# A written, pinned matrix-engine order for the stick-breaking attention of a two-block model

## The chip, the cores and the metric

The kernel runs on one core of a Trainium2 chip. The metric is the device time of one execution, in microseconds (us). The engines of the core work side by side, each through its own queue in order: TensorE (PE, matrix products; PEld is its weight load), VectorE (DVE), ScalarE (ACT), GpSimd (POOL) and SyncE (SP, which issues the transfers).

## The reference

Two transformer-like blocks on 512 tokens of width 1024, in float32. The change lies in the mixer of the second block, in its stick-breaking attention with 16 heads of 64:

```python
def stick_breaking_attention(q, k, v):   # (B, H, S, Dh)
    # A[t,s] = beta_ts * prod_{s<j<t}(1-beta_tj), s<t
    for i in range(s_ // SB_BLOCK):      # blocks of 128 query rows
        z = jnp.einsum('bhtd,bhsd->bhts', qb, kb) * scale
        log_1mb = jnp.where(causal, jax.nn.log_sigmoid(-z), 0.0)
        suffix = lax.cumsum(log_1mb, axis=3, reverse=True) - log_1mb
        log_a = jnp.where(causal, jax.nn.log_sigmoid(z) + suffix, -jnp.inf)
        a = jnp.exp(log_a)
        outs.append(jnp.einsum('bhts,bhsd->bhtd', a, vb))
...
    o_att = rmsnorm(stick_breaking_attention(heads(q), heads(k), heads(v)), attn_norm_g)
    return jnp.concatenate([o_att, o_ssd], axis=-1) @ w_out
```

## The kernel before

Every large product is made of split operands: a float32 number is kept as a high and a low part (`whi`, `wlo` for weights, `a_hi`, `a_lo` for activations) in a format that PE multiplies fast, and three products (high by high, low by high, high by low) are summed in one bank of PSUM. `split` (L79) makes the high part on ACT (L82, or L85 with a factor) and the low part on DVE (L83, or L86). `wload` (L102) fetches a piece of a weight matrix through SP into one of three `raw` buffers and splits it; `whi` and `wlo` have two buffers each.

The attention goes by eight pairs of heads. For each pair `proj_T` makes Q and K, transposed, from the activations: 8 steps of 3 matmuls of 512 columns each (L164), 48 matmuls for a pair, into the banks mm 0 and 1. Q and K are split (L85, L86 and L82, L83) into qh, ql, kh, kl and put into place by 12 transfers on SP (L1056, L1059). Then come three units of query rows (`GROUPS`: blocks 0 and 1 together, block 2, block 3). A unit has, for each of two heads, the scores (L1070, high and low K; for the third unit 512 columns each), a sigmoid l on ACT (L1074), and a running product E along the keys on DVE (L1079, a scan). A unit's E is then turned by PE transposes in float32 (L1087), copied out of PSUM as aT by ACT for the first head and by DVE for the second (L1094, L1096, L1098), and multiplied with V (L1027, values, float32) into the bank `ob`. The values of a unit are held back and issued after the transposes of the next one, so that the float32 products of PE come together in a run; `after` adds dependences that keep it so. The first head's transposes go to a bank `tp`, the second's to bank mm 3. The third unit's values close a pair: ACT adds a row (oaF, L1035) and squares it (q2, L1040), DVE sums the squares (sq, L1041).

V is stored as differences of neighbouring tokens: SP fetches the rows shifted by one into a buffer (L960, L961, L966) and DVE subtracts (L967). Two buffers serve the four row tiles.

After the last pair, zs (the output of the other half of the mixer, of L971 to L983) is transposed on PE (L236) and split, and `w_out` follows in chunks of 24 matmuls (L209, 512 columns each), eight for each half of the output's columns. Of a half's eight, the first four use the transposed zs (a_hi, a_lo) and the others the attention output (oat_hi, oat_lo), which needs the norm over all heads: the sum of squares over partitions (L1111), L1115 to L1120, and for each pair of heads a product on DVE (L1124) and a split.

The order of each engine's instructions is set before the run by a scheduler that takes the instructions in the written order and moves them where its own estimate finds a gap; an instruction marked `keep_in_program_order` isn't moved past others so marked. At run time each engine keeps its order and waits where an operand or a buffer isn't ready.

## Time and profile before

| | |
|---|---|
| time, median of 3 runs | 1955.44 us (1954.67 to 1955.9) |
| the profiled execution | 1953.41 us, its span 1951.6 us |
| PE busy | 1903.7 us, 98% of the span |
| PE weight load busy | 1556.5 us, 80% |
| DVE busy | 982.8 us, 50% |
| ACT busy | 721.8 us, 37% |
| the stick-breaking stretch, first to last score | about 1153.7 to 1310 us of the span |

The span is the time from the first to the last instruction of the profiled execution. A busy PE is not PE at its peak, since matmuls overlap and their ends are modelled. The granted clock is that of PE: 1.00 is 2.4 GHz and 0.50 is 1.2 GHz. Idle time of an engine is named with the instruction that ended it.

### The profile page before, as it was taken

To read this page: it belongs to the slowest core of one execution; us is meant where nothing else is said; L and a number is where in the kernel's file an instruction comes from. 1 tells how busy PE (TensorE), PEld (TensorE's weight loads), DVE (VectorE), ACT (ScalarE), POOL (GpSimd) and SP (SyncE) were. 2 spreads that over 40 slices of the span, in tenths; PEclk is the share of its full clock that TensorE was granted. 3 is DMA by queue.
4 is the path that set the end of the run, shared out by engine and by line. 5 is a ranking of instruction groups with operands and counts; after the bars stand their busy time and mean duration, and the time that the engine had idled before them with its cause. 6 is when DMAs were issued, how large, how long until landed. Compare 5 with 4: busy or idle time off the path is not lost.

```text
span 1951.6 us, 24228 instructions
## 1 busy us (share of the span) xinstructions
PE 1903.7 (98%) x9677; PEld 1556.5 (80%) x9677; DVE 982.8 (50%) x1681; ACT 721.8 (37%) x1246; POOL 38.3 (2%) x66
## 2 busy tenths in 40 slices
PE   7999999999999999999999999999999999999998
PEld 6778888788878888888877877767788888888887
DVE  5578833724553333324668755665464553333223
ACT  4345533233333323223445434544353432323221
POOL 0000000100000000000000000000000000000000
PEclk9999999999999999999999999999999999999999
DMA  7411133232332333333321445442262312333322
GB/s 245 130 44 34 34 97 97 87 98 86 108 97 87 98 97 97 98 97 119 89 82 50 128 121 136 128 120 76 87 194 78 105 57 86 97 98 97 97 97 86
DMA packets 154336, 193.21 MB, mean 99 GB/s; under 512 B 9976, under 2 KB 111732, under 8 KB 154096
## 3 DMA queue, kind: packets, MB, share of 16 engines
q1 hardware_dynamic: 154224, 191.66, 32.7%
q8 instruction: 76, 1.25, 0.3%
q14 instruction: 36, 0.29, 0.0%
HBM read 174.85 MB, written 2.10 MB: 91 GB/s over the span
## 4 chain that ended last, share of the span: by engine, by line
PE 84%; DVE 8%; ACT 1%; issue 1%; POOL 1%; DMA 1%; POOLq 0%; DVEq 0%; ACTq 0%
PE mm L164 43%; PE mm L209 27%; PE mm L187 3%; DVE E L1079 1%; DVE x_sb L279 1%; POOL rp_r L76 1%; PE ob L538 1%; DVE h L251 1%; PE ob L1027 1%; PE s L561 1%; PE ob L924 1%; PE s L1182 1%; PE s L1070 1%; DVE fg L272 1%; PE mm L579 1%
## 5 line engine op out<-in xcount | busy, mean ns | idle before, releaser
L83 DVE TENSOR_TENSOR wlo<-raw,whi 128x1024 fp32r<-128x1024 f32 (+1 forms) x274 | 333.6, 1218 | 680.3 <-ACT whi L82 675.0
L82 ACT ACTIVATE whi<-raw 128x1024 fp32r<-128x1024 f32 (+1 forms) x274 | 289.0, 1055 | 687.3 <-PE mm L164 289.9
L164 PE MATMUL mm<-a_hi,wlo 128*128 128x512 f32 x1120 | 438.0, 391 | 1.6 <-DVE wlo L83 1.6
L164 PE MATMUL mm<-a_hi,whi 128*128 128x512 f32 x1120 | 438.9, 392 | 0.0
L164 PE MATMUL mm<-a_lo,whi 128*128 128x512 f32 x1120 | 438.5, 392 | 0.0
L164 PEld LDWEIGHTS mm<-a_hi,wlo 128*128 128x128 f32 x1120 | 210.3, 188 | 44.5 <-DVE wlo L83 2.0
L164 PEld LDWEIGHTS mm<-a_lo,whi 128*128 128x128 f32 x1120 | 210.3, 188 | 44.0 <-issue 2.4
L164 PEld LDWEIGHTS mm<-a_hi,whi 128*128 128x128 f32 x1120 | 210.3, 188 | 43.3 <-issue 1.4
L209 PE MATMUL mm<-whi,a_hi 128*128 128x512 f32 (+1 forms) x384 | 151.2, 394 | 2.3 <-ACT a_hi L82 2.3
L209 PE MATMUL mm<-whi,a_lo 128*128 128x512 f32 (+1 forms) x384 | 151.7, 395 | 0.0
L209 PE MATMUL mm<-wlo,a_hi 128*128 128x512 f32 (+1 forms) x384 | 150.0, 391 | 0.0
L209 PE MATMUL mm<-whi,hid_hi 128*128 128x512 f32 x288 | 112.0, 389 | 0.0
L209 PE MATMUL mm<-whi,hid_lo 128*128 128x512 f32 x288 | 112.0, 389 | 0.0
L209 PE MATMUL mm<-wlo,hid_hi 128*128 128x512 f32 x288 | 112.0, 389 | 0.0
L209 PEld LDWEIGHTS mm<-whi,a_hi 128*128 128x128 f32 x384 | 72.9, 190 | 19.0 <-ACT a_hi L82 3.1
L209 PEld LDWEIGHTS mm<-whi,a_lo 128*128 128x128 f32 x384 | 72.9, 190 | 15.4 <-issue 2.5
L209 PEld LDWEIGHTS mm<-wlo,a_hi 128*128 128x128 f32 x384 | 72.8, 190 | 14.5 <-issue 1.8
L76 POOL TENSOR_TENSOR rp_r<-rp_a,half 128x1 f32<-128x1 f32 (+1 forms) x58 | 36.9, 636 | 1887.5 <-DVE rp_a L74 1565.0
L209 PEld LDWEIGHTS mm<-whi,hid_lo 128*128 128x128 f32 x288 | 54.1, 188 | 11.3
L209 PEld LDWEIGHTS mm<-wlo,hid_hi 128*128 128x128 f32 x288 | 54.1, 188 | 11.2
L209 PEld LDWEIGHTS mm<-whi,hid_hi 128*128 128x128 f32 x288 | 54.1, 188 | 11.2
L1079 DVE TENSOR_TENSOR_SCAN E<-l,own 128x128 f32<-128x128 f32 (+2 forms) x64 | 48.6, 809 | 10.9 <-ACT l L1074 10.9
(452 smaller groups left out, 2844.8 us busy)
## 6 DMA issues: line engine op xcount, KB each, us to landing
raw<-in_w_in_dram SPq DMA_DIRECT2D x96, 512.0 KB, 3.8
raw<-in_ffn_w_gu_dram SPq DMA_DIRECT2D x88, 512.0 KB, 3.6
raw<-in_ffn_w_down_dram SPq DMA_DIRECT2D x44, 512.0 KB, 3.7
raw<-in_w_out_dram SPq DMA_DIRECT2D x24, 512.0 KB, 3.7
raw<-in_xa_wkv_dram SPq DMA_DIRECT2D x16, 512.0 KB, 4.3
raw<-in_w_ret_o_dram SPq DMA_DIRECT2D x8, 512.0 KB, 3.4
K<-kh SPq DMA_DIRECT2D x32, 128.0 KB, 2.3
K<-kl SPq DMA_DIRECT2D x32, 128.0 KB, 2.3
```

The source lines that it names most:

```text
L76: POOL.tensor_tensor(r[:, :n], a[:, :n], half[:, :n], op=ALU.pow)
L82: ACT.activation(hi, src, AF.Copy)
L83: V.tensor_tensor(lo, src, hi.bitcast(F32), op=ALU.subtract)
L164: PE.matmul(o, a, b, start=(kc + k == 0 and n == 0 and si == 0), stop=(kc + k == K - 1 and n == 2), skip_group_check=True)
L187: PE.matmul(banks[g][j][:, t0 * 128:t1 * 128], a, b, start=(kc + k + n + si == 0), stop=(kc == 1 and k == 3 and n == 2), skip_group_check= ...
L209: PE.matmul(banks[t][:, :w], a, b, start=(kk == 0 and n == 0), stop=(kk == K - 1 and n == 2))
L251: V.scalar_tensor_tensor(h, src, r, g, op0=ALU.mult, op1=ALU.mult)
L272: V.tensor_tensor(fgt, bank, gpost[:, hf * 512:(hf + 1) * 512], op=ALU.mult)
L279: V.scalar_tensor_tensor(xs, fg[:, t if q == 0 else NT + t % 2], r, xs, op0=ALU.mult, op1=ALU.add)
L538: m = PE.matmul(ob[64 * e:64 * e + 64, a], vv[:, j, br, g * 64:(g + 1) * 64], pT[:, e, j], start=False, stop=(br == 1 and j == nk - 1), sk ...
L561: PE.matmul(sbs[e], qS[:, h, qsl], kk[:, br, g, :W], start=(n == 0 and (e == 0 or nk > 2)), stop=(n == 1), skip_group_check=True)
L1079: last = V.tensor_tensor_scan(E[:, rev], l[:, rev], own1[:, 511:(511 - W) if W < 512 else None:-1], 1.0, op0=ALU.mult, op1=ALU.max)
```

## The change

Three things are changed.

First, V's differences get four buffers in place of two (two of them in a free region, `bcT`), and the subtractions are written behind the two steps that make z, two behind each.

Second, the PE instructions of pairs 0 to 6 are written in the order in which they are to run and pinned in it (`pe` marks matmuls and transposes). A generator `projections` yields after each 3 projection matmuls. 28 of its steps go ahead of the first score (Q and K of pair 0, Q of pair 1, half of K of pair 1). Then `ORDER` is followed for each pair: `s` is the scores of one unit and head, `R` a run (the transposes of a unit's two heads, and the values of the unit before), `.` three projection matmuls, sixteen of them in a pair. The third unit's scores stand behind the first unit's run.

Third, pair 7 isn't pinned; there the dependences of `after` stay. The projections end in pair 6.

```diff
@@ -953,19 +953,15 @@
             return f
         for c in range(2):
             proj_X(w, 2048 + c * 512, 512, get, ev_v(c))
-        vbefore = lambda t: d1.tile([128, D], F32, name="vbefore", tag=("xdt", "xdec")[t % 2])
-        vb = vbefore(0)
-        V.memset(vb[0:1], 0.0)
+        vb2 = d1.tile([128, 2, D], F32, name="vb2", tag="bcT")
+        vb = [d1.tile([128, D], F32, name="vb0", tag="xdt"), d1.tile([128, D], F32, name="vb1", tag="xdec"), vb2[:, 0], vb2[:, 1]]
+        V.memset(vb[0][0:1], 0.0)
         for t in range(NT):
-            nc.sync.dma_start(vb[1:113], vv[0:112, t])
-            nc.sync.dma_start(vb[113:128], vv[112:127, t])
-            nxt = None
+            nc.sync.dma_start(vb[t][1:113], vv[0:112, t])
+            nc.sync.dma_start(vb[t][113:128], vv[112:127, t])
             if t < NT - 1:
                 nc.sync.dma_start(vl[t * 8 + 8:t * 8 + 16], vv[127:128, t].rearrange("o (p c) -> o p c", p=8))
-                nxt = vbefore(t + 1)
-                nc.sync.dma_start(nxt[0:1], vv[127:128, t])
-            V.tensor_tensor(vv[:, t], vb, vv[:, t], op=ALU.subtract)
-            vb = nxt
+                nc.sync.dma_start(vb[t + 1][0:1], vv[127:128, t])
 
 
         zs = l1.tile([128, NT, D], F32, name="zs", tag="u3")
@@ -987,6 +983,8 @@
             return t[:, 0], t[:, 1]
         for g in range(2):
             proj_X(w, 3072 + g * 512, 512, get, ev_z(g), tail=2, slots=[spare])
+            for t in range(2 * g, 2 * g + 2):
+                V.tensor_tensor(vv[:, t], vb[t], vv[:, t], op=ALU.subtract)
         tp = tpp.tile([128, 4, 128], F32, name="tp")
         PE.transpose(tp[:, 0, 0:32], vl, ident[0:32, 0:32])
         vlT = l1.tile([128, NT, 8], F32, name="vlT")
@@ -1024,8 +1022,8 @@
                 for i, j, n, o in pv:
                     for e in range(2):
                         h = 2 * p + e
-                        m = PE.matmul(ob[64 * e:64 * e + 64, i * 128:(i + n) * 128], vv[:, j, h * 64:(h + 1) * 64], aTs[e][:, o:o + n],
-                                      start=(i == 0), stop=(n == 2 or j == i), skip_group_check=True)
+                        m = pe(PE.matmul(ob[64 * e:64 * e + 64, i * 128:(i + n) * 128], vv[:, j, h * 64:(h + 1) * 64], aTs[e][:, o:o + n],
+                                         start=(i == 0), stop=(n == 2 or j == i), skip_group_check=True))
                         if first:
                             after(m, *others)
                             first = False
@@ -1041,67 +1039,109 @@
                         V.tensor_tensor(sq, sq, q2, op=ALU.add)
             return f
 
+
+        pinned = [True]
+
+        def pe(m):
+            return tc.keep_in_program_order(m) if pinned[0] else m
+        QK = {}
+
+        def projections():
+
+            for p in range(8):
+
+                Q = qk.tile([128, 2, 512], F32R, name="Q")
+                K = [qk.tile([128, 2, 512], F32R, name=f"K{i}") for i in range(2)]
+                QK[p] = Q, K
+                for nm, c0, scale in (("q", 0, 0.125), ("k", 1024, None)):
+                    hi = a1.tile([128, 512], F32R, name=f"{nm}h")
+                    lo = a1.tile([128, 512], F32R, name=f"{nm}l")
+                    wh, wl = wload(w, 0, 8, c0 + p * 128, 128)
+                    o = bank((0, 1))
+                    for k in range(8):
+                        xh, xl = get(k, 0, NT)
+                        for n, (a, b) in enumerate(((wh, xh), (wh, xl), (wl, xh))):
+                            pe(PE.matmul(o, a[:, k], b, start=(k + n == 0), stop=(k == 7 and n == 2), skip_group_check=True))
+                        if k == 7:
+                            split(hi, lo, o, scale)
+                            for r in range(2):
+                                for e in range(2):
+                                    rows = slice(64 * e, 64 * e + 64)
+                                    if nm == "q":
+                                        nc.sync.dma_start(Q[64 * r:64 * r + 64, e].bitcast(F32), (hi, lo)[r][rows].bitcast(F32))
+                                    else:
+                                        for i, x in enumerate((hi, lo)):
+                                            nc.sync.dma_start(K[i][64 * r:64 * r + 64, e].bitcast(F32), x[rows].bitcast(F32))
+                        yield
+        stream = projections()
+
+        def steps(n):
+            for _ in range(n):
+                next(stream, None)
+
+        def score(p, segs, e):
+
+            Q, K = QK[p]
+            T = segs[-1][1] + (segs[-1][0] + 1) * 128
+            sb = score_bank(p)
+            first = True
+            for i, off in segs:
+                W = (i + 1) * 128
+                for n, k in enumerate(K):
+                    pe(PE.matmul(sb[:, off:off + W], Q[:, e, i * 128:(i + 1) * 128], k[:, e, :W], start=first, stop=(n == 1),
+                                 skip_group_check=True))
+                    first = False
+            l = a2.tile([128, 512], F32, name="l", bufs=3)
+            ACT.activation(l[:, :T], sb[:, :T], AF.Sigmoid, scale=-1.0)
+
+            E = a2.tile([128, 512], F32, name="E", bufs=5)
+            for off, W in (((0, 128), (128, 256)) if len(segs) == 2 else ((0, T),)):
+                rev = slice(off + W - 1, (off - 1) if off else None, -1)
+                last = V.tensor_tensor_scan(E[:, rev], l[:, rev], own1[:, 511:(511 - W) if W < 512 else None:-1], 1.0,
+                                            op0=ALU.mult, op1=ALU.max)
+            return E, last
+
+        def turned(p, segs, Es, last):
+
+            n = segs[-1][1] // 128 + segs[-1][0] + 1
+
+            own, rest = (slice(0, 3, 2), slice(1, 2)) if len(segs) == 2 else (slice(n - 1, n), slice(0, n - 1))
+            aTs = []
+            for e in range(2):
+                tp = tpp.tile([128, 4, 128], F32, name="tp") if e == 0 or p == 7 else bank((3,)).rearrange("p (j q) -> p j q", j=4)
+                for j in range(n):
+                    m = pe(PE.transpose(tp[:, j], Es[e][:, j * 128:(j + 1) * 128], ident))
+                    if e + j == 0 and not pinned[0]:
+                        after(m, last)
+                aT = a2.tile([128, 4, 128], F32, name="aT", bufs=4)
+                (V.tensor_copy if e else ACT.copy)(aT[:, rest], tp[:, rest])
+                if e:
+                    V.tensor_scalar(aT[:, own], tp[:, own], -1.0, None, op0=ALU.add)
+                else:
+                    ACT.activation(aT[:, own], tp[:, own], AF.Identity, bias=less1)
+                aTs.append(aT)
+            if held:
+                held.pop()(*(() if pinned[0] else (last,)))
+            if segs is GROUPS[0]:
+                obs[0] = op_.tile([128, 512], F32, name="ob")
+            held.append(values(p, segs, aTs, obs[0]))
+        obs = [None]
+        steps(28)
+
+        ORDER = "sss.s..Rs.sR...R.........".replace(" ", "")
         for p in range(8):
-
-            Q = qk.tile([128, 2, 512], F32R, name="Q")
-            K = [qk.tile([128, 2, 512], F32R, name=f"K{i}") for i in range(2)]
-            for nm, c0, scale in (("q", 0, 0.125), ("k", 1024, None)):
-                hi = a1.tile([128, 512], F32R, name=f"{nm}h")
-                lo = a1.tile([128, 512], F32R, name=f"{nm}l")
-                proj_T(w, c0 + p * 128, 128, get, lambda j, bank, hi=hi, lo=lo, sc=scale: split(hi, lo, bank, sc), of=(0, 1))
-                for r in range(2):
-                    for e in range(2):
-                        rows = slice(64 * e, 64 * e + 64)
-                        if nm == "q":
-                            nc.sync.dma_start(Q[64 * r:64 * r + 64, e].bitcast(F32), (hi, lo)[r][rows].bitcast(F32))
-                        else:
-                            for i, x in enumerate((hi, lo)):
-                                nc.sync.dma_start(K[i][64 * r:64 * r + 64, e].bitcast(F32), x[rows].bitcast(F32))
-            ob = None
-            for segs in GROUPS:
-                T = segs[-1][1] + (segs[-1][0] + 1) * 128
-                css, last = [], None
-                for e in range(2):
-                    sb = score_bank(p)
-                    first = True
-                    for i, off in segs:
-                        W = (i + 1) * 128
-                        for n, k in enumerate(K):
-                            PE.matmul(sb[:, off:off + W], Q[:, e, i * 128:(i + 1) * 128], k[:, e, :W], start=first, stop=(n == 1),
-                                      skip_group_check=True)
-                            first = False
-                    l = a2.tile([128, 512], F32, name="l", bufs=3)
-                    ACT.activation(l[:, :T], sb[:, :T], AF.Sigmoid, scale=-1.0)
-
-                    E = a2.tile([128, 512], F32, name="E", bufs=5)
-                    for off, W in (((0, 128), (128, 256)) if len(segs) == 2 else ((0, T),)):
-                        rev = slice(off + W - 1, (off - 1) if off else None, -1)
-                        last = V.tensor_tensor_scan(E[:, rev], l[:, rev], own1[:, 511:(511 - W) if W < 512 else None:-1], 1.0,
-                                                    op0=ALU.mult, op1=ALU.max)
-                    css.append(E)
-
-                aTs = []
-                for e in range(2):
-                    tp = tpp.tile([128, 4, 128], F32, name="tp") if e == 0 or p == 7 else bank((3,)).rearrange("p (j q) -> p j q", j=4)
-                    for j in range(T // 128):
-                        m = PE.transpose(tp[:, j], css[e][:, j * 128:(j + 1) * 128], ident)
-                        if e + j == 0:
-                            after(m, last)
-                    aT = a2.tile([128, 4, 128], F32, name="aT", bufs=4)
-
-                    n = T // 128
-                    own, rest = (slice(0, 3, 2), slice(1, 2)) if len(segs) == 2 else (slice(n - 1, n), slice(0, n - 1))
-                    (V.tensor_copy if e else ACT.copy)(aT[:, rest], tp[:, rest])
-                    if e:
-                        V.tensor_scalar(aT[:, own], tp[:, own], -1.0, None, op0=ALU.add)
-                    else:
-                        ACT.activation(aT[:, own], tp[:, own], AF.Identity, bias=less1)
-                    aTs.append(aT)
-                if held:
-                    held.pop()(last)
-                if ob is None:
-                    ob = op_.tile([128, 512], F32, name="ob")
-                held.append(values(p, segs, aTs, ob))
+            pinned[0] = p < 7
+            todo = [(u, e) for u in range(3) for e in range(2)]
+            ES, runs = {}, list(range(3))
+            for c in ORDER:
+                if c == "s":
+                    u, e = todo.pop(0)
+                    ES[u, e] = score(p, GROUPS[u], e)
+                elif c == "R":
+                    u = runs.pop(0)
+                    turned(p, GROUPS[u], [ES[u, e][0] for e in range(2)], ES[u, 1][1])
+                elif p < 7:
+                    steps(1)
         held.pop()()
         osT = new_act()
         for t in range(NT):
```

On PE, in the second pair of heads (pair 1), from the third unit's scores to the second unit's transposes: `s` and `mm` are score banks, `tp` and `mm` with `E` the transposes of the first and the second head, `ob` the values, `mm<-a_..` the projections. Before:

```order
L1070 MATMUL s<-K_9152,Q 128x512
L1070 MATMUL s<-K_9153,Q 128x512
L1087 MATMUL mm<-cst,E 128x128
L1070 MATMUL mm<-K_9152,Q 128x512
L1087 MATMUL tp<-cst,E 128x128 x3
L1087 MATMUL mm<-cst,E 128x128 x2
L1027 MATMUL ob<-aT,vv 64x128 x8
L1087 MATMUL tp<-cst,E 128x128 x3
L1070 MATMUL mm<-K_9153,Q 128x512
L1087 MATMUL mm<-cst,E 128x128 x3
```

Now, from the first unit's transposes:

```order
L1113 MATMUL tp<-cst,E 128x128 x3
L1113 MATMUL mm<-cst,E 128x128 x3
L1025 MATMUL ob<-aT,vv 64x128 x8
L1091 MATMUL s<-K_9048,Q 128x512
L1091 MATMUL s<-K_9049,Q 128x512
L1064 MATMUL mm<-a_hi,whi 128x512
L1064 MATMUL mm<-a_lo,whi 128x512
L1064 MATMUL mm<-a_hi,wlo 128x512
L1091 MATMUL mm<-K_9048,Q 128x512
L1091 MATMUL mm<-K_9049,Q 128x512
L1113 MATMUL tp<-cst,E 128x128 x3
L1113 MATMUL mm<-cst,E 128x128 x3
```

The third unit's scores moved from ahead of the first unit's transposes to behind its run, with three projection matmuls between their two heads, and the pieces of a run stand together.

On PE, from the third unit's transposes of pair 6 on (`mm<-cst,zs` are the transposes of zs, `mm<-whi,a_hi` and the like matmuls of w_out). Before:

```order
L1087 MATMUL tp<-cst,E 128x128 x4
L1087 MATMUL mm<-cst,E 128x128 x4
L1027 MATMUL ob<-aT,vv 64x128 x6
L164 MATMUL mm<-a_lo,whi 128x512
L164 MATMUL mm<-a_hi,wlo 128x512
L236 MATMUL mm<-cst,zs 128x128 x12
L209 MATMUL mm<-whi,a_hi 128x512
L236 MATMUL mm<-cst,zs 128x128 x8
L209 MATMUL mm<-whi,a_lo 128x512
```

Now:

```order
L236 MATMUL mm<-cst,zs 128x128 x5
L1113 MATMUL tp<-cst,E 128x128 x4
L236 MATMUL mm<-cst,zs 128x128 x3
L1113 MATMUL mm<-cst,E 128x128 x4
L1025 MATMUL ob<-aT,vv 64x128 x6
L236 MATMUL mm<-cst,zs 128x128 x4
L209 MATMUL mm<-whi,a_hi 128x512
L236 MATMUL mm<-cst,zs 128x128 x3
L1091 MATMUL s<-K_10227,Q 128x128
```

The transposes of zs, before all behind the pair's last projection, now begin ahead of the third unit's transposes, and pair 7's first score stands behind 15 of them.

On DVE, behind pair 7: the norm (`rstd`), the scaled heads (`oaF`), their splits (`oat_lo`) and the weight splits of w_out (`wlo`). Before:

```order
L1118 TENSOR_TENSOR rstd<-rstd 128x512
L83 TENSOR_TENSOR memT_lo<-tp,memT_hi 128x512
L1119 SCALAR_TENSOR_TENSOR rstd<-rstd 128x512
L83 TENSOR_TENSOR wlo<-raw,whi 128x1024
L1120 SCALAR_TENSOR_TENSOR rstd<-rstd 128x512
L1124 SCALAR_TENSOR_TENSOR oaF<-oaF,cwT,rstd 128x512 x3
L83 TENSOR_TENSOR oat_lo<-oaF,oat_hi 128x4x128 x2
```

Now:

```order
L1159 SCALAR_TENSOR_TENSOR rstd<-rstd 128x512
L1160 SCALAR_TENSOR_TENSOR rstd<-rstd 128x512
L1164 SCALAR_TENSOR_TENSOR oaF<-oaF,cwT,rstd 128x512 x3
L83 TENSOR_TENSOR oat_lo<-oaF,oat_hi 128x4x128 x3
L1164 SCALAR_TENSOR_TENSOR oaF<-oaF,cwT,rstd 128x512 x4
L83 TENSOR_TENSOR oat_lo<-oaF,oat_hi 128x4x128 x4
L1164 SCALAR_TENSOR_TENSOR oaF<-oaF,cwT,rstd 128x512
L83 TENSOR_TENSOR wlo<-raw,whi 128x1024
```

The weight split that stood between two steps of the norm (chunk 3 of w_out, counted from 0) now stands behind the last scaled head.

## Rows read from the trace of the kernel before

**Rows 1.** The page's part on the chain that ended last.

```profile
PE 84%; DVE 8%; ACT 1%; issue 1%; POOL 1%; DMA 1%; POOLq 0%; DVEq 0%; ACTq 0%
```

**Rows 2.** Windows: length, busy (xcount) of PE, PEld, DVE, ACT, POOL; clock; DMA.

```profile
1153.69:1173.91 20.22, 19.29 (x103) 14.32 (x102) 10.94 (x19) 7.89 (x16) 0.00 (x0) 1.00 0.53 126
...
1256.88:1277.59 20.71, 19.77 (x121) 15.18 (x120) 14.59 (x24) 11.51 (x25) 1.10 (x2) 1.00 0.55 154
1277.59:1300.80 23.21, 19.24 (x116) 14.26 (x115) 14.73 (x24) 10.77 (x24) 0.00 (x0) 0.87 0.62 183
1295.00:1301.00 6.00, 5.31 (x19) 4.14 (x17) 2.77 (x4) 2.07 (x4) 0.00 (x0) 0.50 0.78 214
1135.00:1142.00 7.00, 6.57 (x29) 5.46 (x30) 3.76 (x11) 2.31 (x4) 1.51 (x2) 1.00 0.42 130
1342.00:1346.00 4.00, 4.00 (x12) 3.13 (x11) 1.89 (x3) 0.00 (x0) 0.00 (x0) 0.57 0.55 161
600.00:700.00 100.00, 100.00 (x443) 82.81 (x442) 33.97 (x35) 29.40 (x37) 0.00 (x0) 1.00 0.31 95
1173.91:1256.88 82.97, 79.19 (x482) 60.72 (x480) 47.88 (x76) 37.76 (x84) 0.00 (x0) 1.00 0.53 128
```

**Rows 3.** Timeline at the start: start us, us, engine, line, what.

```profile
1132.94 0.24 PE L991 MATMUL tp<-cst,vl 32*128 32x32 f32 x1
...
1133.46 0.40 PE L164 MATMUL mm<-a_lo,whi 128*128 128x512 f32 x1
...
1135.29 0.68 DVE L977 SCALAR_TENSOR_TENSOR zs<-zs,mm 128x512 f32<-128x512 f32 x1
...
1135.43 0.50 PE L164 MATMUL mm<-a_hi,wlo 128*128 128x512 f32 x1 [1.57 <-DVE wlo L83]
```

**Rows 4.** Timeline of PE in one steady pair.

```profile
1199.80 1.09 PE L1027 MATMUL ob<-aT,vv 128*64 128x128 f32 x16
...
1202.52 0.52 PE L1087 MATMUL mm<-cst,E 128*128 128x128 f32 x3 [0.88 <-DVE aT L1096]
...
1205.74 0.60 PE L1087 MATMUL tp<-cst,E 128*128 128x128 f32 x4
...
1206.71 0.88 PE L1027 MATMUL ob<-aT,vv 128*64 128x128 f32 x12
1207.51 0.50 PE L164 MATMUL mm<-a_lo,whi 128*128 128x512 f32 x1
1207.85 0.40 PE L164 MATMUL mm<-a_hi,wlo 128*128 128x512 f32 x1
```

**Rows 5.** Timeline of PE between pair 6 and pair 7.

```profile
1293.99 1.62 PE L236 MATMUL mm<-cst,zs 128*128 128x128 f32 x8 [2.34 <-DVE kl L83]
1296.30 0.80 PE L209 MATMUL mm<-whi,a_hi 128*128 128x512 f32 x1 [0.69 <-ACT a_hi L82]
```

**Rows 6.** Timeline of PE and DVE in the tail.

```profile
1317.42 1.09 PE L1027 MATMUL ob<-aT,vv 128*64 128x128 f32 x14
...
1329.55 1.22 DVE L83 TENSOR_TENSOR wlo<-raw,whi 128x1024 fp32r<-128x1024 f32 x1
...
1330.68 0.69 DVE L1120 SCALAR_TENSOR_TENSOR rstd<-rstd 128x512 f32<-128x512 f32 x1
...
1340.32 1.22 DVE L83 TENSOR_TENSOR wlo<-raw,whi 128x1024 fp32r<-128x1024 f32 x1
...
1341.60 0.50 PE L209 MATMUL mm<-wlo,oat_hi 128*128 128x512 f32 x1 [1.92 <-DVE wlo L83]
```

**Rows 7.** DVE by line and shape in the four steady pairs: count, busy us, mean ns.

```profile
L1079 DVE TENSOR_TENSOR_SCAN E<-l,own 128x512 f32<-128x512 f32 x8 | 9.7, 1209 | 0.0
...
L1041 DVE TENSOR_TENSOR sq<-sq,q 128x512 f32<-128x512 f32 x3 | 2.0, 681 | 0.0
```

**Rows 8.** Timeline of DVE where V is subtracted.

```profile
1100.74 1.23 DVE L83 TENSOR_TENSOR wlo<-raw,whi 128x1024 fp32r<-128x1024 f32 x1 [3.08 <-ACT whi L82]
```

## The prediction

> **What bounds the kernel now.** I read the chain of work that ended last first: it lies on the matrix engine (PE) for 84% of the span and on the vector engine (DVE) for 8% [rows 1]. So only time that PE gains counts, and a wait of PE on DVE is what can be removed or added. Then the table of windows [rows 2]. In it the reader is to see three kinds of stretch: a pure projection stretch (600 to 700 us), where PE never idles; the four steady pairs, where PE is busy 79.19 of 82.97 us; and pair 6, which takes 23.21 us from its first score to that of pair 7, at a mean granted clock of 0.87. Last the rows of single stretches: the start [rows 3], one steady pair [rows 4], the turn from pair 6 to pair 7 [rows 5] and the tail [rows 6]. The sum is a clock of its own: when each place is reached, before and now. Times are those of the one profiled execution (1953.4 us, span 1951.6); it lies 2.0 us under the median of the runs (1955.4), so 2.0 is added at the end. About 0.2% (3.9 us) is what a measurement of this kernel can tell from no change.
>
> **Start.** Before, PE begins the first K projection while the bank of the first Q projection is still read; after two matmuls it idles 1.57 us on the DVE split and goes on at 1135.43 [rows 3]. The written order puts Q first, and its bank is free only when the DVE product that starts at 1135.29 and takes 0.68 ends. So the first matmul starts at about 1136.0 with none done. The lead that the change names is hardly new: 84 projection matmuls stand before the first score now, 82 before. One matmul takes 0.226 (443 in 100 us [rows 2]), so the first score comes at 1136.0 + 84 x 0.226 = 1155.0, against 1153.69.
>
> **A steady pair.** The work, piece by piece. 48 projection matmuls: 10.85. Scores: two heads of 2560 columns, at 512 columns in 0.226: 2.26. Transposes: 8 take 0.97 with one change of format [rows 4], so 0.11 each and 2.2 for 20. Values: 1.09 for 16 [rows 4], 0.80 for 12, and 0.8 taken for the first unit's 8: 2.7. A change between the two formats costs 0.11 (the first matmul after the values takes 0.34, not 0.23 [rows 4]); the new order has three runs of float32 work, six changes: 0.66. Together 18.7. The 20.74 of before (82.97 over 4 [rows 2]) are this, the 0.88 us in which PE waits for the DVE copy of the transposes [rows 4], and 1.2 of more changes and small weight-load waits.
> What is late next? In the new order the third unit's second head is the critical one: its transposes need a bank that DVE empties, and in DVE's queue stand ahead of that copy a scan of 512 (1.21), the sum of squares (0.68), a K split of the same size and a second scan of 512 (1.21) [rows 7]. Counted through, the copy ends some 11.5 us into the pair, and PE is there at 11.2. I take 0.3 of wait; the bounds are 0 and the 0.88 of now [rows 4]. Period 19.0, bounds 18.7 to 19.5: a gain of 1.7 (1.2 to 2.0), four times.
> Pair 0 has no values of an earlier pair in its first run (1.09 less): 17.9 against 20.22 [rows 2]. Pair 5 also carries two normalisation steps of the memory rows, which the table shows as 14.59 us of DVE [rows 2] against 47.88 / 4 = 12.0 in the others; in the new order they stand ahead of scans that PE waits for. I take 20.7, no gain, with 19.4 and 22 as bounds.
> So pair 6's first score comes at 1155.0 + 17.9 + 4 x 19.0 + 20.7 = 1269.6, before 1277.59.
>
> **Pair 6 to pair 7.** Before, projections end the pair, and then PE has nothing ready: the transposes of zs wait 2.34 us for a K split on DVE, then 0.69 us for ScalarE (ACT) [rows 5], and afterwards the clock is at 0.50 (the 1.2 GHz level) until about 1301 [rows 2]. Now only 12 projection matmuls are left in pair 6, and zs transposes fill the gaps between its runs. The work is 12 x 0.226 = 2.7, scores 2.3, runs 4.9, changes 1.1, 15 zs transposes 1.7 and one matmul of w_out 0.2: 12.9. The waits move: PE stands about 0.7 us for ACT's split of the third zs block and 1.2 us for DVE's of the second, which are queued behind a weight split and the last copies, with 0.3 as in a pair. That makes 15.2, and pair 7's first score at 1284.8, before 1300.80. Pair 7 is left to the scheduler and keeps its 17.7 us (last value product before: 1317.42 + 1.09 = 1318.5 [rows 6]): last value at 1302.5, 16.0 us earlier. K of pair 7 is issued late enough to land at about the time when it is wanted; 1 us either way.
>
> **Tail.** What was done at the boundary must be done later: of w_out's first eight chunks 17 matmuls are done before the last value now, 24 before. And DVE's order in the tail has moved. Before, the weight split of chunk 3 went just ahead of the last step of the norm, at 1329.55, so it was long done; PE's wait was 1.92 us on chunk 4's split, which stood behind the eight scaled pairs of heads and six of their splits [rows 6]. Now chunk 3's own split stands behind the eight and seven of their splits. In times after the last value: the last norm step started at 12.2 [rows 6] and starts 1.1 earlier without the split; from it to the weight split were 9.64 [rows 6], now one split (0.6) more; the split takes 1.22: PE can go on at 22.6. It gets there with 63 matmuls instead of 80, so 17 x 0.227 = 3.9 earlier than before (1341.60 - 1.92 = 1339.68, that is 21.2): at 17.3. A new wait of 5.3 us. At the end of the wait 104 matmuls were done at 23.1 before, and 80 at 22.6 now; the 24 missing cost 5.4. Of the 16.0 us remain 16.0 + 0.5 - 5.4 = 11.1.
>
> **Clock.** Two waits of before ended in a half-clock stretch: the 2.34 with 0.69 behind it, and the 1.92 of the tail, which is followed by 4 us at 0.57 [rows 2]; 4 x 0.43 = 1.7 lost. The 1.57 at the start did not: 1.00 from 1135 to 1142 [rows 2]. The start now waits from 1133.2, where the last small matmul ends [rows 3], to 1136.0, 2.8 us, longer than either: I take one loss of 1.7 (0 to 3.4). The two waits at pair 6's end stand close together and make 1.9: 1.7 again (0 to 3.4). The 5.3 of the tail lose about 2.2 against 1.7 before: 0.5 (-0.7 to 1.7). Together 3.9, which leaves 11.1 - 3.9 = 7.2.
>
> **Edits with no price.** The four differences of V get four buffers, so two run back to back and the loads of V go out ahead of two weight loads on SP's queue. DVE idles 3.08 us just there [rows 8], which hides the second 1.22; without that cover it would be 1.2 once. Pinning itself adds no instruction.
>
> **A page against the rows.** PE is busy in the steady pairs for 79.19 of 82.97 us, so of idle time at most 3.78 us, 0.95 a pair, could be won; the rest of my 1.7 are changes of format, which the trace counts as busy [rows 2, 4]. Weight loads are busy 60.72 of the 82.97 us, 0.732, and 0.828 in the projection stretch [rows 2]. The Trainium skill, "Perfetto Trace Analysis", section "Identifying the Most-Contended Engine", says that matmul busy time is no good measure of the room left on this engine, and that the share of weight loads is one. The trace agrees in so far as a matmul after a change takes longer and is yet counted as busy. By busy time alone the sum would be 3.0 us less (four pairs at 0.95 instead of 1.7); what the other share would give is worked out as the second rival.
>
> **Rivals.**
> *DVE keeps the wait.* If the copy for the third unit comes as late as the 0.88 of now and the runs stall on their scans too, a pair gains 0.6 instead of 1.7. For: DVE has the two scans, sum and split in one line. Against: DVE is busy only 12 of 20.7 us. Five pairs lose 1.1 each: gain 1.7, median 1953.7, no change that can be told.
> *Pairs as dense as projections.* If a pair packs its weight loads like the projection stretch, the period is 20.74 x 0.732 / 0.828 = 18.3. Five pairs gain 0.7 more: 10.7 in all, 1944.7. Against: short transposes and values cannot be packed like 512 columns.
> *Half clock inside the pairs (slower).* In a pinned pair the first 13 us have only 7 x 3 long matmuls between short ones, and nothing else may fill a wait. If each of pairs 1 to 6 loses one stretch like that of 1342 to 1346, 6 x 1.7 = 10.2 go: 3.0 us slower, 1958.4. It decides from five pairs (8.5 against 7.2). For: 1295 to 1301 was such a thin stretch, at 0.50 [rows 2]. Against: the pairs of before have the same pieces with a wait of 0.88, at 1.00.
> *It does not do what it says.* The order is pinned on PE alone, so that it comes out is certain; the lead of one and three quarter pairs is not new (84 against 82), so no gain can come from it. That is in the sum already.
>
> **How the numbers follow.** Forecast: 1953.4 - 7.2 = 1946.2 profiled, 1948.2 as median; its own bounds are 1943 to 1954. Chances: forecast 0.52, DVE keeps the wait 0.20, dense pairs 0.14, half clock in the pairs 0.14. Faster by over 0.2% means under 1951.5: 0.46 of the forecast, the dense pairs and 0.03 of the first rival, 0.63. Same: 0.05, 0.17 and 0.01, 0.23. Slower: 0.14. The range must take in the dense pairs and most of the DVE case and of the bounds: 1941.5 to 1957.
>
> **What would show it.** First scores 19.0 us apart and no wait over 0.4 at the third unit's transposes; first score at 1155 and last value near 1304 to 1306; waits of about 0.7 and 1.2 at pair 6's end; PE waiting about 5 us on a weight split near 1322; granted clock 1.00 in pairs 0 to 5 and a dip after the start. I am wrong if the pairs stay above 20 us, if the clock dips inside them, or if the tail's wait is missing.

## The result and the profile after

The changed kernel takes 1944.47 us, median of 4 runs (1944.11 to 1947.88); the kernel before, timed beside it, 1955.67 (1954.67 to 1960.36). The ratio is 0.9942, 95% interval 0.9922 to 0.9961: faster by about 11 us, 0.6%. The profiled executions give 1944.22 (span 1942.4) against 1953.41 (span 1951.6), 9.2 us.

The page of after, the chain that ended last, to compare with [rows 1]:

```profile
PE 85%; DVE 7%; POOL 1%; ACT 1%; issue 1%; DMA 1%; SPq 0%; POOLq 0%; DVEq 0%; ACTq 0%
```

DVE gave one per cent of the chain to PE. Windows of after, with columns as in [rows 2]: pair 0, pairs 1 to 4, pair 5, pair 6 (each from its first score to the next pair's), then the tail behind its wait.

```profile
1156.67:1174.71 18.04, 17.92 (x106) 14.59 (x105) 11.29 (x19) 7.81 (x16) 0.00 (x0) 1.00 0.71 175
1174.71:1250.83 76.12, 76.12 (x481) 61.89 (x480) 46.63 (x76) 38.52 (x86) 0.00 (x0) 1.00 0.56 139
1250.83:1271.11 20.28, 19.24 (x122) 15.45 (x121) 14.40 (x24) 10.45 (x24) 1.09 (x2) 1.00 0.64 182
1271.11:1285.84 14.73, 13.09 (x102) 10.38 (x100) 11.77 (x21) 9.38 (x22) 0.00 (x0) 1.00 0.64 169
1326.00:1331.00 5.00, 4.65 (x12) 3.70 (x13) 2.03 (x3) 0.00 (x0) 0.00 (x0) 0.54 0.59 158
```

Four pairs take 76.12 us in place of 82.97, and PE never idles in them. Pair 6 takes 14.73 in place of 23.21, at full clock. The tail goes on at 0.54. What PE waits for in after, between 1130 and 1345 (total us, times, longest):

```profile
PE mm L209 <- DVE wlo L83: 5.4, 1, 5.4
PE mm L1064 <- DVE zs L973: 2.8, 1, 2.8
PE mm L1113 <- DVE aT L1119: 1.7, 2, 1.0
PE mm L209 <- ACT a_hi L82: 0.7, 1, 0.7
PE ob L1025 <- DVE E L1100: 0.6, 1, 0.6
PE mm L236 <- DVE kl L83: 0.3, 1, 0.3
PE mm L236 <- DVE a_lo L83: 0.2, 1, 0.2
```

The last value product ends at 1303.68, 14.8 us earlier than before (1318.51, [rows 6]). 5.6 of them are given back behind it: from there to the end of the span after takes 638.72 us, before 633.09. So most of the 8.5 us by which pair 6 is shorter go again in the tail: pairs 0 to 5 win 9.5 us, the start loses 3.1, and from pair 6 on 2.7 are won.

**The measure of the experiments.** The medians of different kernels here carry a scatter of a few us that the edits don't explain: the stretch before the small matmul `tp<-cst,vl`, in which PE's order is the same in all of them, ended between 1132.35 and 1138.10 us in the profiled executions (the last section shows what goes with it). So beside the median each kernel is told by stages from that small matmul on, read from the trace: to the first score, the pairs, pair 7 to the end of its last value, from there to the first w_out matmul that takes the attention output, and the rest. "Sum" is all of these. Each ratio is to runs of the kernel before on the same chip beside it; their medians were 1957.12 for `e1_start`, `e2_tail`, `e8_both` and `e4_unpinned`, 1955.32 for `e3_vv_only`, `e6_switch`, `e9_third` and `e7_lead24`, and 1953.63 for the other three.

| kernel | to first score | pair 0 | pairs 1 to 4, mean | pair 5 | pair 6 | pair 7 | last value to `oat_hi` | rest | sum | median |
|---|---|---|---|---|---|---|---|---|---|---|
| before | 20.75 | 20.22 | 20.74 | 20.71 | 23.21 | 17.71 | 19.14 | 613.95 | 818.7 | 1955.67 |
| after | 23.83 | 18.04 | 19.03 | 20.28 | 14.73 | 17.84 | 28.42 | 610.30 | 809.6 | 1944.47 |
| e3_vv_only | 20.74 | 20.22 | 20.72 | 20.72 | 22.93 | 17.98 | 19.13 | 613.85 | 818.5 | 1956.23 |
| e4_unpinned | 22.78 | 18.16 | 19.03 | 20.70 | 15.17 | 17.85 | 28.33 | 610.59 | 809.7 | 1946.18 |
| e9_third | 23.87 | 17.78 | 19.02 | 19.01 | 13.77 | 19.02 | 29.01 | 610.29 | 808.8 | 1945.02 |
| e6_switch | 22.27 | 17.78 | 19.01 | 19.05 | 13.48 | 18.10 | 28.01 | 610.53 | 805.3 | 1945.62 |
| e7_lead24 | 22.38 | 21.36 | 22.31 | 25.62 | 26.04 | 17.60 | 19.13 | 612.07 | 833.4 | 1972.64 |
| e7_lead30 | 25.18 | 18.66 | 18.95 | 20.23 | 11.90 | 18.54 | 28.61 | 610.30 | 809.2 | 1946.62 |
| e1_start | 19.36 | 18.06 | 19.03 | 20.34 | 14.70 | 17.70 | 28.67 | 610.36 | 805.3 | 1942.72 |
| e2_tail | 23.84 | 18.05 | 19.03 | 20.70 | 14.73 | 17.85 | 20.74 | 610.28 | 802.3 | 1938.59 |
| e8_both | 19.42 | 18.93 | 19.03 | 20.58 | 14.71 | 17.70 | 21.14 | 610.46 | 799.1 | 1933.27 |
| e10_all | 19.36 | 17.76 | 19.01 | 19.05 | 13.48 | 18.09 | 21.38 | 610.45 | 795.6 | 1932.95 |
| e11_all_third | 19.38 | 17.78 | 19.04 | 19.30 | 14.75 | 19.02 | 20.95 | 610.55 | 797.9 | 1932.40 |

### The profile page after: what moved, and what is told of

It reads as the page before. It is cut to its first block, busy times and chain, and to the rows that moved or that the text cites. A ratio compares the mean times of both kernels' runs of the same rounds, so it can differ in the third digit from the quotient of the medians.

```text
span 1942.4 us, 24240 instructions
## 1 busy us (share of the span) xinstructions
PE 1896.9 (98%) x9677; PEld 1558.4 (80%) x9677; DVE 980.0 (50%) x1681; ACT 721.5 (37%) x1246; POOL 38.6 (2%) x66
## 4 chain that ended last, share of the span: by engine, by line
PE 85%; DVE 7%; POOL 1%; ACT 1%; issue 1%; DMA 1%; SPq 0%; POOLq 0%; DVEq 0%; ACTq 0%
PE mm L164 39%; PE mm L209 28%; PE mm L1064 4%; PE mm L187 3%; POOL rp_r L76 1%; DVE x_sb L279 1%; PE ob L538 1%; PE ob L1025 1%; DVE h L251 1%; PE s L561 1%; PE ob L924 1%; PE s L1091 1%; PE s L1222 1%; DVE a_lo L83 1%; DVE fg L272 1%
## 5 line engine op out<-in xcount | busy, mean ns | idle before, releaser
L164 PE MATMUL mm<-a_hi,whi 128*128 128x512 f32 x992 | 388.6, 392 | 0.0
L164 PE MATMUL mm<-a_hi,wlo 128*128 128x512 f32 x992 | 387.5, 391 | 0.0
L164 PE MATMUL mm<-a_lo,whi 128*128 128x512 f32 x992 | 387.0, 390 | 0.0
L164 PEld LDWEIGHTS mm<-a_hi,whi 128*128 128x128 f32 x992 | 186.3, 188 | 39.1 <-issue 1.2
L164 PEld LDWEIGHTS mm<-a_hi,wlo 128*128 128x128 f32 x992 | 186.3, 188 | 38.4 <-issue 0.2
L164 PEld LDWEIGHTS mm<-a_lo,whi 128*128 128x128 f32 x992 | 186.3, 188 | 38.0 <-issue 0.3
L209 PEld LDWEIGHTS mm<-wlo,hid_hi 128*128 128x128 f32 x288 | 54.1, 188 | 11.2
L209 PEld LDWEIGHTS mm<-whi,hid_lo 128*128 128x128 f32 x288 | 54.1, 188 | 11.2
```

The source lines that it names most:

```text
L164: PE.matmul(o, a, b, start=(kc + k == 0 and n == 0 and si == 0), stop=(kc + k == K - 1 and n == 2), skip_group_check=True)
L209: PE.matmul(banks[t][:, :w], a, b, start=(kk == 0 and n == 0), stop=(kk == K - 1 and n == 2))
```

## The experiments

**The two losses of the changed kernel.** The theory of the prediction is that the pairs win some 16 us and that two waits, at the start and in the tail, take part of it back, each with a half-clock stretch behind it. Three kernels take these waits away.

*The start.* `e1_start`:

```diff
-                    o = bank((0, 1))
+                    o = bank((1, 0))
```

> The changed kernel (1944.5 median, 1944.2 profiled) with the two projection banks taken in the other order, so that the first Q projection goes into the bank whose last reader is long done. Theory: the 2.8 us in which the matrix engine stands before the first Q matmul go, and with them the 1.7 us that the stretch at granted clock 0.66 behind them loses (1135 to 1142); the first K projection then needs the other bank 5.4 us later, when its reader is done. First score 4.4 us earlier (1152.2), everything behind it shifted by as much, profiled 1939.8, median about 1940. Rival A: the weight split of Q takes the place of the bank, the wait stays and the time is within 1 us of 1944.5. Rival B: the idle time goes but the clock dips all the same: 2.8 us less, 1941.7.

In after, PE at the start (columns as in [rows 3], the wait in brackets); then the same place in this kernel:

```profile
1132.84 0.25 PE L989 MATMUL tp<-cst,vl 32*128 32x32 f32 x1
1135.90 0.68 PE L1064 MATMUL mm<-a_hi,whi 128*128 128x512 f32 x1 [2.82 <-DVE zs L973]
1136.38 0.63 PE L1064 MATMUL mm<-a_lo,whi 128*128 128x512 f32 x1
```

```profile
1134.70 0.25 PE L989 MATMUL tp<-cst,vl 32*128 32x32 f32 x1
1134.87 0.50 PE L1064 MATMUL mm<-a_hi,whi 128*128 128x512 f32 x1
1135.21 0.40 PE L1064 MATMUL mm<-a_lo,whi 128*128 128x512 f32 x1
```

The 2.82 us are gone and no wait took their place; the matmuls go at 0.23 us each at once, where in after the first eight went at 0.43. From the small matmul to the first score it is 19.36 in place of 23.83, 4.5 us against 4.4 expected, and nothing behind it changed. Theory held by the stages. The median, 1942.72 (ratio 0.9930, 0.9916 to 0.9945), moved by less than 4.5 and can't show it alone: the profiled execution came to the small matmul 1.9 us later than after did.

*The tail.* `e2_tail`; `between` is called between the chunks of w_out's first half:

```diff
-        for k in range(8):
-            V.scalar_tensor_tensor(oaF[:, k], oaF[:, k], cwT[:, 60 + k:61 + k], r0, op0=ALU.mult, op1=ALU.mult)
-            split(oaT[0][:, :, k], oaT[1][:, :, k], oaF[:, k].rearrange("p (t q) -> p t q", t=NT))
+        def scaled(ch):
+            if ch in (3, 4, 5):
+                for k in {3: range(4), 4: (4, 5), 5: (6, 7)}[ch]:
+                    V.scalar_tensor_tensor(oaF[:, k], oaF[:, k], cwT[:, 60 + k:61 + k], r0, op0=ALU.mult, op1=ALU.mult)
+                    split(oaT[0][:, :, k], oaT[1][:, :, k], oaF[:, k].rearrange("p (t q) -> p t q", t=NT))
```

> The changed kernel with the scaled heads of the attention output written between the chunks of w_out that don't need them: pairs 0 to 3 behind chunk 3, 4 and 5 behind chunk 4, 6 and 7 behind chunk 5, so that the vector engine makes the weight split of chunk 3 ahead of them. Theory: the wait of 5.4 us at 1326.35 goes and the half-clock stretch behind it (1325 to 1335) with its 2.0 us: 7.3 us less, profiled 1936.9, median about 1937. Rival A: the wait moves to chunk 4's split, as in the kernel before (1.9 us of wait and 1.7 of clock): 3.7 us less, about 1941. Rival B: the chain of the norm is the bound, the engine waits for the heads themselves instead, and no more than 2 us are won.

DVE in after, from the last step of the norm on: the weight split of chunk 3 stands behind eight scaled heads (L1164) and seven of their splits, and PE waits for it.

```profile
1314.83 0.69 DVE L1160 SCALAR_TENSOR_TENSOR rstd<-rstd 128x512 f32<-128x512 f32 x1
1315.55 2.08 DVE L1164 SCALAR_TENSOR_TENSOR oaF<-oaF,cwT,rstd 128x512 f32<-128x512 f32 x3
...
1324.41 0.74 DVE L1164 SCALAR_TENSOR_TENSOR oaF<-oaF,cwT,rstd 128x512 f32<-128x512 f32 x1
1325.08 1.22 DVE L83 TENSOR_TENSOR wlo<-raw,whi 128x1024 fp32r<-128x1024 f32 x1
1326.35 0.79 PE L209 MATMUL mm<-wlo,a_hi 128*128 128x512 f32 x1 [5.42 <-DVE wlo L83]
```

DVE in this kernel: chunk 3's split behind one scaled head, chunk 4's behind four.

```profile
1321.27 0.75 DVE L1167 SCALAR_TENSOR_TENSOR oaF<-oaF,cwT,rstd 128x512 f32<-128x512 f32 x1
1321.94 1.22 DVE L83 TENSOR_TENSOR wlo<-raw,whi 128x1024 fp32r<-128x1024 f32 x1
...
1326.87 1.22 DVE L83 TENSOR_TENSOR wlo<-raw,whi 128x1024 fp32r<-128x1024 f32 x1
```

Its windows from the last value to the first attention matmul, and from there on:

```profile
1309.38:1330.12 20.74, 20.74 (x98) 16.68 (x98) 15.87 (x23) 13.85 (x22) 0.00 (x0) 1.00 0.19 56
1330.12:1345.00 14.88, 14.88 (x65) 12.00 (x64) 7.31 (x9) 4.90 (x6) 0.00 (x0) 1.00 0.28 100
```

PE doesn't idle at all and keeps its clock: 20.74 us in place of 28.42, 7.7 against 7.3 expected. Neither chunk 4 nor the norm took the wait over, so both rivals fall. The median is 1938.59 (ratio 0.9905, 0.9887 to 0.9922).

*Both.* `e8_both`, the two diffs together:

> Both edits, the banks at the start and the scaled heads between the chunks of the tail, in the changed kernel. Theory: the two places are 170 us apart and the matrix engine is busy 98% of the span, so the gains add up: 4.4 + 7.3 = 11.7 us, profiled 1932.5, median about 1932.8, ratio to the kernel before 0.988. Rival: an earlier start of the pairs is taken back by something with a time of its own (transfers of weights for w_out, the norm's chain), and the sum is worth no more than the larger of the two, about 1937.

1933.27 (ratio 0.9884, 0.9866 to 0.9902); the profiled execution also 1933.27. The gains add up: 10.5 us by the stages, 11.2 by the medians. Against 11.7 expected, 0.9 us went in pair 0: its first eight score matmuls took 1.79 us in place of the 0.92 of `e1_start`, and the wait among them was for the transfer of K.

**What makes the pairs shorter.** The change does several things to them at once: a written order, a pin, another place for the third unit's scores, another lead. First, where the time went. Added up over pairs 1 to 4, each instruction counted until the next one starts, a mean pair of before is 11.77 us of projections, 3.16 of scores, 2.24 of transposes, 2.70 of values and the wait of 0.88; of after it is 11.21, 2.64, 2.54 and 2.63 with no wait. So half of the 1.7 us is the wait, and the other half are scores and projections that take less in the new order, where PE goes over between the float32 work (transposes and values) and the other format six times in a pair, before ten times.

*The pin.* `e4_unpinned`:

```diff
-        pinned = [True]
+        pinned = [False]
...
-            pinned[0] = p < 7
+            pinned[0] = False
```

> The changed kernel with no instruction pinned: the same written order, the same steps of projections between runs, but the scheduler is free to move, with the dependences of the kernel before in place of the pin. Theory (the writing does it, the pin only keeps it): the matrix engine's order in pairs 0 to 5 stays nearly the same, so first scores stay 19.0 us apart and the time is within 1.5 us of 1944.5. Rival (the pin does it): the scheduler moves scores and runs apart again, pairs come back to 20.7 us, and the time goes back to 1953 to 1956.

Pairs 1 to 4 take 19.03 us as with the pin, the sum of the stages is 809.7 against 809.6, the median 1946.18 (ratio 0.9945, 0.9927 to 0.9962). In these pairs PE's order is that of after, instruction by instruction, so the order as written does it; without the pin the dependences of `after` are back, and with them the scheduler leaves it alone. It does move the start: PE's first matmuls come there in the order of the kernel before, and PE waits 1.56 us on a weight split in place of 2.82 on the bank.

*V alone.* `e3_vv_only` is the kernel before with the first part of the diff, four buffers and the subtractions behind the z steps:

```diff
             proj_X(w, 3072 + g * 512, 512, get, ev_z(g), tail=2, slots=[spare])
+            for t in range(2 * g, 2 * g + 2):
+                V.tensor_tensor(vv[:, t], vb[t], vv[:, t], op=ALU.subtract)
```

> The kernel before with the first part of the change alone: V's differences get four buffers and are subtracted behind the two steps that make z. Theory: no price and no gain, since the subtractions lie in idle time of the vector engine; the stretch up to the first projection and the pairs stay as they are (20.7 us each, 23.2 in pair 6), time within 1.5 us of the kernel before. Rival: the earlier transfers or the subtractions shift the vector engine's queue at the start, so that the first Q projection waits for its bank as in the changed kernel: first score 3 us later (23.8 in place of 20.8 us after the last small matmul), time 3 us more.

20.74 us to the first score and 20.72 a pair, as before; ratio 1.0008 (0.9995 to 1.0020). This part by itself has no price and no gain, and the wait of 2.82 at the start is not its doing: by `e1_start` it is the bank that Q is given, the one that is read last.

*The third unit's place.* `e9_third` puts its scores ahead of the first unit's run again:

```diff
-        ORDER = "sss.s..Rs.sR...R.........".replace(" ", "")
+        ORDER = "sss.s..ssR....R...R......".replace(" ", "")
```

> The changed kernel with the third unit's scores written ahead of the first unit's run again, as they stood in the kernel before; everything else stays pinned. Theory (the place of the third unit does not matter much, the projections between the runs hide the copies): pairs stay at 19.05 us or lose up to 0.3 each to a wait at the third unit's transposes: within 2 us of 1944.5. Rival (its place is what removed the vector engine's wait): two scans of 1.2 us stand ahead of the first unit's copies again, the wait of 0.9 us per pair comes back, first scores 19.9 to 20.0 apart, 5 to 6 us more: 1950.

Its windows for pairs 1 to 4 and for pair 5:

```profile
1178.74:1254.80 76.06, 76.06 (x482) 61.93 (x481) 47.74 (x76) 38.91 (x86) 0.00 (x0) 1.00 0.56 139
1254.80:1273.81 19.01, 19.01 (x122) 15.48 (x120) 14.39 (x24) 10.37 (x23) 1.09 (x2) 1.00 0.56 153
```

19.02 a pair and no wait. So the place that the change gives to the third unit isn't what removed the wait of 0.88. What the two orders share, and before lacks in places, is projection matmuls between one run and the next; no kernel took those away by themselves, so that they are the reason is likely and not shown. The old place is even better in pair 5, where after waits 1.04 us for the copy of the third unit and this kernel for nothing, and it loses 1.2 in pair 7. The sum is 808.8, the median 1945.02 (ratio 0.9953, 0.9937 to 0.9969): the same.

*Changes of format.* `e6_switch` puts three projection matmuls between the transposes and the values of each run and takes them from the end of the pair:

```diff
             if held:
+                if p < 7:
+                    steps(1)
                 held.pop()(*(() if pinned[0] else (last,)))
...
-        ORDER = "sss.s..Rs.sR...R.........".replace(" ", "")
         for p in range(8):
+            ORDER = "sss.s..Rs.sR...R......" + ("." if p == 0 else "")
```

> The changed kernel with three projection matmuls put between the transposes and the values of each run that has values, and taken away from the end of the pair: the same work, but the matrix engine changes its format twice more for each run. Theory (a change of format costs 0.11 us): six more changes in a pair, 0.66 us, first scores 19.7 us apart in place of 19.05, and some 4 us more in all (18 runs): 1948.5. Rival A (changes cost nothing, the gain of a pair was the wait alone): first scores stay 19.05 apart and the time within 1 us of 1944.5. Rival B: the values wait less for the copies than the changes cost, pairs come to under 19.0.

The expectation failed: pairs take 19.01, not 19.7, which is the time that rival A gave for changes that cost nothing. PE in the second unit's run, first after, then this kernel (start, duration; matmuls overlap, so the distance from start to start is what counts):

```profile
1181.90 0.49 PE L1113 MATMUL tp<-cst,E 128*128 128x128 f32 x3
1182.23 0.49 PE L1113 MATMUL mm<-cst,E 128*128 128x128 f32 x3
1182.65 0.87 PE L1025 MATMUL ob<-aT,vv 128*64 128x256 f32 x8
1183.45 0.50 PE L1064 MATMUL mm<-a_hi,whi 128*128 128x512 f32 x1
1183.79 0.40 PE L1064 MATMUL mm<-a_lo,whi 128*128 128x512 f32 x1
```

```profile
1181.50 0.49 PE L1113 MATMUL tp<-cst,E 128*128 128x128 f32 x3
1181.82 0.49 PE L1113 MATMUL mm<-cst,E 128*128 128x128 f32 x3
1182.07 0.47 PE L1064 MATMUL mm<-a_hi,whi 128*128 128x512 f32 x1
1182.38 0.40 PE L1064 MATMUL mm<-a_lo,whi 128*128 128x512 f32 x1
1182.62 0.40 PE L1064 MATMUL mm<-a_hi,wlo 128*128 128x512 f32 x1
1182.94 0.87 PE L1025 MATMUL ob<-aT,vv 128*64 128x256 f32 x8
1183.75 0.50 PE L1064 MATMUL mm<-a_hi,whi 128*128 128x512 f32 x1
```

A projection matmul behind transposes or on either side of the values takes 0.31 to 0.34 from start to start in place of 0.23, 0.08 to 0.11 more. But three transposes take 0.42 when values follow them, 0.33 when transposes do and 0.25 when a projection matmul does. So the edit pays 0.08 and 0.09 on two projection matmuls and gets 0.17 back on the transposes: from the first head's transposes to the end of the values it is 1.55 without the three projection matmuls and 2.25 with them, which are 0.69 by themselves. The six changes that it adds to a pair cost nothing in sum, so 0.11 for each is no price that adds up; what PE does at such a border the rows don't tell. The stages win 4.3 us all the same (805.3), in other places: the wait of pair 5 is gone (19.05), pair 6 takes 13.48. 1.6 of the 4.3 are the stretch to the first score, where this execution kept its clock. The profiled execution, 1940.62, is the fastest of four, the others take 1945.44 to 1946.69; the median is 1945.62 (ratio 0.9950, 0.9932 to 0.9969), so it shows none of that.

*The lead.* `e7_lead24` and `e7_lead30`:

```diff
-        steps(28)
+        steps(24)
```

> The changed kernel with 24 steps of projections ahead of the first score in place of 28 (one and a half pairs). Theory: the next pair's K is then finished only at the eighth of the sixteen steps of a pair, 24 matmuls of 0.226 us (5.4 us) ahead of the scores that need it, while splitting it and moving it take about 9 us; the matrix engine waits some 3.6 us for the transfer in each of pairs 1 to 6, with the clock falling behind each of these waits: 20 us more or worse, 1965 or above. Rival (the lead has slack): K is there in time, the pairs stay at 19.05 and the time within 1.5 us of 1944.5.

```diff
-        steps(28)
+        steps(30)
```

> The changed kernel with 30 steps of projections ahead of the first score in place of 28. Theory (28 is enough, K of the next pair lands long before its scores): first scores stay 19.05 apart, the first score comes 6 matmuls (1.4 us) later and pair 6 is as much shorter; time within 1 us of 1944.5. Rival A (a longer lead is what shortens a pair): pairs under 18.9, over 1 us less. Rival B (pair 6 lacks the six matmuls as cover and its waits grow): 1 to 2 us more, all of it in pair 6.

With 24 steps it is 1972.64 (ratio 1.0093, 1.0073 to 1.0114), 28 us slower than after. Its PE at the first scores of a pair, and then its window of pairs 1 to 4:

```profile
1181.02 0.30 PE L1091 MATMUL s<-K,Q 128*128 128x128 f32 x1 [0.90 <-issue]
1181.66 0.95 PE L1091 MATMUL s<-K,Q 128*128 128x128 f32 x4 [0.35 <-DMA K<-kl]
```

```profile
1181.02:1270.24 89.22, 82.59 (x480) 65.00 (x481) 48.10 (x75) 38.11 (x85) 0.00 (x0) 0.96 0.49 119
```

The pieces of K land one by one while PE asks for them. 6.63 us of idle time in four pairs are 1.7 a pair, half of the 3.6 expected; the rest of the 3.3 by which a pair is longer is matmuls that run slower beside the waits and at a mean clock of 0.96. Direction and place were right, the split between wait and clock was not. The largest single loss is pair 6, 26.04 in place of 14.73, at a mean clock of 0.77. With 30 steps the first score comes 1.35 later, six matmuls of 0.226, pair 6 is 2.8 shorter (1.4 were expected) and pair 7 0.7 longer, pairs 1 to 4 take 18.95, and the sum is 809.2, as after's; 1946.62 (ratio 0.9960, 0.9948 to 0.9972). So 28 is enough, and a longer lead isn't what shortens a pair.

**A version that is faster still.** `e10_all` is `e8_both` with the edit of `e6_switch`; `e11_all_third` has the third unit's place of `e9_third` as well:

```diff
-            ORDER = "sss.s..Rs.sR...R......" + ("." if p == 0 else "")
+            ORDER = "sss.s..ssR....R...R..." + ("." if p == 0 else "")
```

> Three edits in the changed kernel: banks at the start, scaled heads between the chunks of the tail, and three projection matmuls between the transposes and the values of a run. Measured alone in their own stretches they gave 4.5 us (lead 23.8 to 19.4), 7.7 us (last value to first attention matmul 28.4 to 20.7) and 2.6 us (first score of pair 0 to last value 147.0 to 144.4). Theory: they add up, 14.8 us under the changed kernel's 1944.5: 1929.7, and 3 us under the kernel with the first two alone. Rival: the third is worth nothing once the pairs start 4.5 us earlier (K of pair 1 lands late, as pair 0 of the kernel with the first two edits already showed 18.9 in place of 18.0): 1932 to 1933.

> The same with the third unit's scores written ahead of the first unit's run. Theory: within 1 us of the kernel with the three edits (pairs of 19.0 us in every order so far; pair 7, which took 19.0 with this order in place of 17.8, loses 1 us). Rival: with all scores ahead, the copies of the first unit come behind two long scans and a wait of 0.9 us per pair is back: 5 us more.

1932.95 (ratio 0.9895, 0.9878 to 0.9912) and 1932.40 (0.9892, 0.9877 to 0.9907). By the stages the first wins 3.5 us over `e8_both` (795.6 against 799.1; 3 were forecast), the second 1.2. The medians don't show them: they lie at 1932 to 1933, where the rival for the first had put it, and not at 1929.7. Part of that is seen: the profiled execution of `e10_all` came to the small matmul at 1136.00, that of `e8_both` at 1132.35. Whether the stages' gain would show in more runs stays open. What is shown is that removing the two waits takes the kernel to about 1933, 1.2% under the kernel before (`e8_both`).

## Why the prediction was right

The forecast was 7.2 us of gain in the profiled execution, 1948.2 as median; measured are 9.2 and 1944.47, inside the range. The number alone doesn't decide for the forecast: the rival of dense pairs gave 1944.7 and 10.7 us, and that is as near. What decides is where the time went. The forecast added 2.0 us from the profiled execution to the median, as before; in after the two lie 0.25 apart, so of the median's 11.2 us of gain some 2 are scatter. Step by step:

- **Start.** Wait 2.8 forecast, 2.82 measured; first score at 1155.0 plus 1.7 for the clock, that is 1156.7, measured 1156.67. `e1_start` showed both parts to be one place's. The wait was worked out; that the clock fell behind it in this execution was luck, since in `e6_switch` it did not (last section).
- **Steady pair.** 19.0 forecast, 19.03 measured. The makeup differs: there is no wait of 0.3, PE is busy 76.12 of 76.12 us. In its place pairs 1 to 4, from start to start, give scores 2.64 (2.26 forecast by columns) and transposes 2.54 (2.2), and projections with their changes of format 11.21 where 10.85 + 0.66 were taken. Two terms were 0.7 too small and one 0.3 too large, and by `e6_switch` the price of 0.11 for each change was no sound term: that these errors cancel is luck.
- **The wait of 0.88.** It went, as forecast. The count of DVE's queue has the copy that frees the third unit's bank end 11.5 us into the pair, and PE there at 11.2. In pair 2 of after, which begins at 1193.65, the copy ends at 11.29 and the transposes start at 11.44:

```profile
1204.66 0.28 DVE L1119 TENSOR_SCALAR aT<-mm 128x128 f32<-128x128 f32 x1
1205.09 0.63 PE L1113 MATMUL mm<-cst,E 128*128 128x128 f32 x4
```

That is 0.15 behind the copy's end, as in pair 5, where PE was waiting; so the copy still sets the time here, and costs about 0.07 (the first head's four transposes take 0.51, in pair 1, where no sum of squares stands in DVE's queue, 0.44). But the third unit's place doesn't decide it, since the wait stays away with that unit in its old place (`e9_third`).
- **Pair 5.** 20.7 forecast, 20.28 measured, with a wait of 1.04 on the copy of the third unit, which two other orders don't have.
- **Pair 6.** 15.2 of work and waits forecast, 14.73 measured. The 15.2 counted waits of 0.7, 1.2 and 0.3; the rows below show 0.69 on ACT as forecast, 0.64 at the third unit's transposes and 0.31 on a split of K. The wait on DVE's split of zs, 1.2 forecast, is 0.24 and comes behind pair 7's first score (1285.84).

```profile
1280.81 0.33 PE L236 MATMUL mm<-cst,zs 128*128 128x128 f32 x1 [0.31 <-DVE kl L83]
1282.55 0.63 PE L1113 MATMUL mm<-cst,E 128*128 128x128 f32 x4 [0.64 <-DVE aT L1119]
1285.25 0.50 PE L209 MATMUL mm<-whi,a_hi 128*128 128x512 f32 x1 [0.69 <-ACT a_hi L82]
1289.19 0.33 PE L236 MATMUL mm<-cst,zs 128*128 128x128 f32 x1 [0.24 <-DVE a_lo L83]
```

- **Clock.** The term that was mis-sized. 1.7 us were taken for a dip behind pair 6's waits; the clock stayed at 1.00 through pair 6 (window above) and through pair 7. This is most of the 2.0 us by which the gain exceeds the forecast; pair 5 and pair 6's own 0.4 and 0.5 make the rest, and pair 0, pair 7 and the tail take back 0.5 together.
- **Tail.** Wait 5.3 forecast, 5.42 measured; PE goes on 22.6 after the last value, measured 1326.35 - 1303.68 = 22.67. Price of the tail with its clock 5.4, measured 638.72 - 633.09 = 5.6. `e2_tail` showed the cause to be the place of one weight split in DVE's queue.
- **The lead.** That it holds no gain is shown from both sides: 30 steps win nothing and 24 lose 28 us.
- **The rivals.** DVE does not keep the wait. Half clock inside the pairs did not come: 1.00 in all of them. Dense pairs, at 18.3 a pair from the share of weight loads, did not come either, in any of the orders tried with a sufficient lead: 18.95 to 19.04. That the median lies at their 1944.7 is chance. The weight loads are busy 61.89 of 76.12 us, 0.813, short of the 0.828 of the projections.
- **Busy time as a measure.** The Trainium skill, "Perfetto Trace Analysis", section "Identifying the Most-Contended Engine", says that matmul busy time is no good measure of the room left on this engine. The trace agrees: before, PE was busy 79.19 us in the four pairs [rows 2], and after they take 76.12 in all, so 3.07 us of busy time were won.

## What to carry to other kernels

Where an engine is busy nearly all the time, keep a clock by places (when is each stage reached, before and now), and count for each engine what stands ahead of the one instruction that the bound engine will ask for next: both losses of this change, a bank at the start and a weight split behind eight products in the tail, could be read from the order, and each was removed by a few lines. Write an order so that the bound engine has independent work between a copy and its use; whether the order is pinned, and which of several such orders it is, mattered little here. Where runs of one kernel scatter by more than an edit is worth, compare stages of the trace that begin behind the scatter.
